# Experts' tokens normed behind their first product, second top-16 searches beside the key searches: a change to a hybrid encoder layer on one core

## The chip, the core and the metric

The kernel runs on one core of one Trainium2 chip. Time is device time in microseconds (us), the median of several timed runs. The profile is one further execution with the hardware profiler on; the engines are called as it calls them: PE (TensorE, with its weight loads as PEld), DVE (VectorE), ACT (ScalarE), POOL (GpSimd) and SP (SyncE, which issues most DMAs here).

## What is computed

One layer on 256 tokens of width 2048: an RMS norm, a combined projection, a bidirectional RWKV-7 group and a grouped-query attention group, an output projection, and then a product-key mixture of single-neuron experts, which is the part that the change touches:

```
h2 = rmsnorm(x, norm2_w)                       # 256 tokens x 2048
q = (h2 @ w_pq).reshape(T, 8, 2, 128)          # 8 heads, two halves each
s = einsum('thpc,hpnc->thpn', q, sub_keys)     # 128 keys per half
s1, i1 = top_k(s[:, :, 0], 16)                 # first searches: keys
s2, i2 = top_k(s[:, :, 1], 16)
cand = s1[..., :, None] + s2[..., None, :]     # 16 x 16 sums
best, ci = top_k(cand, 16)                     # second search
e1 = take_along_axis(i1, ci // 16); e2 = take_along_axis(i2, ci % 16)
expert = e1 * 128 + e2
gate = softmax(best)
act = gelu(h2 . u_tab[expert]) * gate
out = sum over experts of act * v_tab[expert]  # then x + out, and a last rmsnorm
```

The kernel does not gather experts. It multiplies all tokens with all 16384 rows of `u_tab`, weighs the Gelu of the result with a dense gate matrix that is zero where an expert wasn't chosen, and multiplies with all of `v_tab`.

## The kernel before, in words

The first third of the time (to about 635 us) holds the projections, the RWKV and attention groups and most of the output projection; their order comes from a scheduler, and the change does not touch it. From there on the order is written out by hand: a list `todo` of pieces, each one load of 512 KB of weights (128 partitions x 1024 values), and a function `go()` (line 764) that brings the next piece. `go()` issues loads some six pieces ahead, splits pieces three ahead, and then runs the products of the piece that is due. Splitting means that ACT rounds the raw weights to a part `wH` and that either POOL or DVE subtracts it from the raw values, which leaves `wL` (`split_piece`, line 750). Which engine subtracts is the third member of a piece. Tokens are split likewise, and three products (high x high, high x low, low x high) give a product of nearly full precision. What stands between two calls of `go()` is put on the engines' queues between the pieces. Each engine runs its own queue in order.

The pieces, in order:

1. Eight late pieces of the output projection (`late`, line 787). Behind each 128-wide chunk of `x2` (the residual, channels on partitions) ACT makes the high part of chunk times norm weight, `pH`, and DVE the remainder `pL` (`rest`, line 806). The squares go to the sum for the RMS norm.
2. 32 pieces of queries, two for each of 16 half-heads (`query`, line 821), from `pH` and `pL`, so without the token's RMS factor, which is applied to the key scores (`scores_of`, line 841) as ACT's scale. POOL subtracts. Each score block is searched by DVE for its 16 largest (`search`, line 849; `top16`, line 832: two rounds of eight maxima, their indices, and a replacement). In the same loop `h2_chunk` (line 929) makes the tokens for the experts: DVE multiplies a chunk with the norm weight and with the RMS factor spread over all partitions (`rb2`), ACT rounds it to the high half of `hh`, DVE subtracts for the low half.
3. 256 pieces of up-projection (`up`, line 856): each pair gives 128 experts x 256 tokens, in PSUM as one product of 512 columns (high and low tokens side by side) and one of 256. ACT copies the low half out into a buffer `S`, DVE adds the other half. There are 26 buffers of two such results (`NSB`).
   - Over the first 28 of these pieces (`ROUTE`) run the lookups (`route`, line 986): DVE makes the 80 sums that can hold the 16 largest of the 16 x 16, in three instructions for eight heads, searches them (the second search), finds row and column, and looks the experts' numbers up by comparing (`oh`), multiplying with a copy of the index lists that ACT spreads (`ex`), and adding in a tree of halves; then the softmax. One half of the tokens (b = 0, 1) follows the other. `turn` (line 979) transposes the residual back between pieces. POOL subtracts in this stretch, DVE in the next 64 pieces.
   - Over the 64 pieces behind these the dense gates are made (`hot`, `gate`, lines 1086 and 1097): DVE makes one-hot rows, PE multiplies them, ACT copies, SP stores them to memory.
4. 16 groups of 16 down-projection pieces (`down`, line 874), with the remaining up pieces between the first ten groups. `ready` (line 1165) prepares the next group in steps between pieces: Gelu on ACT, weighing with the gates on DVE (`weigh`), rounding on ACT, remainder on DVE (`remain`). The gates of a group are loaded back by SP (`gate_load`, line 1142). In groups 11 to 15 no up pieces are left. One piece in three is subtracted by DVE, the others by POOL.
5. The last norm and the stores (`finish`).

Of the kernel before, what the change touches and what calls it, by code (L numbers as in the profile page):

```python
# [37 lines left out]
ROUTE = 28  # L38
RSTEPS = 22
# [95 lines left out]
def body(tc, a, out, dbg={}):  # L135
# [592 lines left out]
    accp = pool("accp", side="right")  # L728
    tk = pool("tk", side="right")
    skp = pool("skp", side="right")  # L730
    x2p = pool("x2p", side="right")
    pH = x2p.tile([128, 16, 256], R, name="pH")
    pL = x2p.tile([128, 16, 256], R, name="pL")
# [53 lines left out]
    def late(m):  # L787
# [4 lines left out]
        def use(raw):  # L792
            for n in (2 * m, 2 * m + 1):
# [6 lines left out]
                act(pH[:, n], x2(n), AF.Copy, scale=Pm("n2", n))  # L800
# [5 lines left out]
    def rest(n):  # L806
        V.scalar_tensor_tensor(pL[:, n], x2(n), Pm("n2", n), pH[:, n].bitcast(F), op0=OP.mult, op1=OP.subtract)  # L807
# [45 lines left out]

    Sb, upp = {}, {}

    def up(i, j, c, eng):
        def use(H, L):
# [3 lines left out]
            for k in range(8):  # L861
                mm(p, H[:, k], hh[:, c + k].rearrange("p x t -> p (x t)"), c + k == 0, False)
                mm(p[:, 0:256], L[:, k], hh[:, c + k, 0], False, c + k == 15)
            if c:
                if not j:
                    Sb[i] = sp.tile([128, 2, 256], F, name="S")
# [39 lines left out]
    for r, (i, j, c) in enumerate(ups[:4 * NSB]):  # L906
        todo.append(up(i, j, c, V if ROUTE <= r < ROUTE + 64 else G))
# [18 lines left out]
    hh = actp.tile([128, 16, 2, 256], R, name="xy")  # L926
    hw = {}

    def h2_chunk(n):
        if n < 16:  # L930
            hw[n] = s2p.tile([128, 256], F, name="w", bufs=3)
            V.scalar_tensor_tensor(hw[n], x2(n), Pm("n2", n), rb2, op0=OP.mult, op1=OP.mult)
# [5 lines left out]
    n_h = 0  # L938
    for n in range(16):
        go()  # L940
        if n == 0:
# [288 lines left out]
```

## Time and profile before

| | us |
|---|---|
| timed runs, median of 3 (lowest to highest) | 2300.5 (2297.33 to 2303.76) |
| the profiled execution | 2296.94 |
| its span, first to last instruction | 2295.2 |
| PE busy in it | 2226.0 |
| DVE / ACT / POOL busy | 1180.9 / 936.7 / 861.7 |
| mean granted TensorE clock | 0.982 of full |

Lines of a profile that begin with two numbers are instructions in order of time: start and duration in us, engine, line of the kernel, operation, what it writes and reads, shapes, and in brackets how long the engine was idle before it and what ended that. In the chain (the work that ended last, followed back) the two numbers are start and length of a run of such work. In a stretch (`A:B`) stand its length, then the busy time and the count of PE, PEld, DVE, ACT and POOL, the granted clock, the share of the DMA engines, and GB/s. In a group stand line, engine, operation, tiles, shapes and count, then total busy us and mean ns of one, then the idle time before them. Many instructions are recorded under the lines of three helpers, 159 (`mm`), 162 (`act`) and 165 (`tt`), so they are told apart by their tiles: `wH` and `wL` are split weights, `oh` and `ee` belong to the lookups, `o` to the gates, `h<-gd` to the loading of the gates.

### The profile page before, as it was taken

Reading aid. Unit: us, or ns where it says so; the run is one execution under the profiler, and the core shown is the slowest. Engines: PE = TensorE matmul, PEld = TensorE weight load, DVE = VectorE, ACT = ScalarE, POOL = GpSimd, SP = SyncE. Lnnn points to the kernel's source line nnn. Section 1 sums busy time; section 2 is a strip of 40 time slices with the busy share of each in tenths; the row PEclk is TensorE's granted clock in tenths of the full one; section 3 lists DMA queues with packets and bytes.
Section 4 is the critical chain, followed back from the end, with each engine's and each line's share of the span. In section 5 each row is a group of like instructions: output and inputs, shape, how many; then the busy total and the mean of one; then the engine's idle time right before and its main releaser. Section 6 shows DMA issues by size and latency. Waiting matters only on the chain.

```text
span 2295.2 us, 33834 instructions
## 1 busy us (share of the span) xinstructions
PE 2226.0 (97%) x13042; PEld 1897.7 (83%) x13042; DVE 1180.9 (51%) x2498; ACT 936.7 (41%) x1350; POOL 861.7 (38%) x393
## 2 busy tenths in 40 slices
PE   8999799899999999999999999999999999999997
PEld 7888688787889878999888888888888888887786
DVE  3364865774468888888532332332322332345544
ACT  1121222223144545555544444444444444444443
POOL 0000000000036780000655555555555555555554
PEclk9999799799999999999999999999999999999999
DMA  5465364366364445666766566566566566676664
GB/s 199 147 192 167 128 193 152 104 205 190 116 204 146 156 164 194 215 217 219 226 197 209 185 206 208 185 209 209 186 203 209 187 207 196 199 224 220 207 205 134
DMA packets 188833, 431.52 MB, mean 188 GB/s; under 512 B 39680, under 2 KB 82304, under 8 KB 184448
## 3 DMA queue, kind: packets, MB, share of 16 engines
q1 hardware_dynamic: 177376, 409.96, 56.2%
q10 hardware_dynamic: 11296, 19.40, 2.5%
q8 instruction: 103, 1.69, 0.3%
q14 instruction: 58, 0.48, 0.1%
HBM read 391.55 MB, written 37.75 MB: 187 GB/s over the span
## 4 chain that ended last, share of the span: by engine, by line
PE 88%; DVE 5%; issue 2%; POOL 2%; DMA 1%; ACT 1%; SPq 0%; POOLq 0%; ACTq 0%
PE pc L159 35%; PE pj L159 32%; PE pr L159 18%; POOL wL L165 2%; PE pt L159 1%; DVE oh L165 1%; PE pr L533 0%; DVE S L165 0%; DMA h<-gd 0%; DMA cst<-cst 0%; ACT wH L162 0%; DVE pk L165 0%; DVE pL L807 0%; DVE o L1093 0%; DVE AK L165 0%
## 5 line engine op out<-in xcount | busy, mean ns | idle before, releaser
L165 POOL TENSOR_TENSOR wL<-raw,wH 128x1024 fp32r<-128x1024 f32 x344 | 836.2, 2435 | 998.4 <-ACT wH L162 990.9
L162 ACT ACTIVATE wH<-raw 128x1024 fp32r<-128x1024 f32 x544 | 575.2, 1060 | 472.2 <-PE pc L159 282.6
L165 DVE TENSOR_TENSOR wL<-raw,wH 128x1024 fp32r<-128x1024 f32 x200 | 250.3, 1252 | 369.2 <-ACT wH L162 368.9
L159 PE MATMUL pc<-wH,aL 128*128 128x512 f32 x1024 | 405.5, 396 | 0.0
L159 PE MATMUL pc<-wH,aH 128*128 128x512 f32 x1024 | 404.0, 395 | 1.2 <-DVE acc L165 1.1
L159 PE MATMUL pc<-wL,aH 128*128 128x512 f32 x1024 | 404.2, 395 | 0.0
L159 PE MATMUL pj<-xy,rw 128*128 128x256 f32 x1664 | 385.4, 388 | 0.2 <-ACT xy L162 0.2
L159 PE MATMUL pr<-xy,wH 128*128 128x512 f32 x1024 | 365.9, 399 | 2.8 <-ACT wH L162 2.8
L159 PE MATMUL pj<-xy,wH 128*128 128x512 f32 x1024 | 364.7, 398 | 0.8 <-ACT wH L162 0.8
L159 PEld LDWEIGHTS pj<-xy,rw 128*128 128x128 f32 x1664 | 318.3, 194 | 50.4 <-issue 4.7
L159 PE MATMUL pr<-xy,wL 128*128 128x256 f32 x1024 | 287.5, 281 | 2.0 <-POOL wL L165 1.9
L159 PE MATMUL pj<-xy,wL 128*128 128x256 f32 x1024 | 286.8, 280 | 1.8 <-POOL wL L165 1.0
L159 PEld LDWEIGHTS pc<-wH,aH 128*128 128x128 f32 x1024 | 192.2, 188 | 49.0 <-DVE acc L165 2.5
L159 PEld LDWEIGHTS pr<-xy,wH 128*128 128x128 f32 x1024 | 192.8, 188 | 46.5 <-ACT wH L162 3.1
L159 PEld LDWEIGHTS pc<-wL,aH 128*128 128x128 f32 x1024 | 192.2, 188 | 46.8
L159 PEld LDWEIGHTS pc<-wH,aL 128*128 128x128 f32 x1024 | 192.2, 188 | 46.1
L159 PEld LDWEIGHTS pj<-xy,wH 128*128 128x128 f32 x1024 | 192.1, 188 | 44.1 <-ACT wH L162 1.1
L159 PEld LDWEIGHTS pr<-xy,wL 128*128 128x128 f32 x1024 | 194.2, 190 | 2.6 <-POOL wL L165 2.6
L159 PEld LDWEIGHTS pj<-xy,wL 128*128 128x128 f32 x1024 | 193.4, 189 | 2.8 <-POOL wL L165 1.3
L165 DVE TENSOR_TENSOR acc<-pc,acc 128x512 f32<-128x512 f32 x128 | 86.3, 688 | 148.5 <-PE pc L159 148.5
L505 POOL COPY vp<-zv 128x256 f32<-128x256 f32 x16 | 8.0, 498 | 307.8 <-PE pr L510 178.8
L162 ACT ACTIVATE gc<-pc 128x512 f32<-128x512 f32 x64 | 68.9, 1077 | 73.6 <-PE pc L159 73.6
(298 smaller groups left out, 2308.6 us busy)
## 6 DMA issues: line engine op xcount, KB each, us to landing
raw<-u SPq DMA_DIRECT2D x256, 512.0 KB, 4.1
raw<-v SPq DMA_DIRECT2D x256, 512.0 KB, 3.9
rw<-win SPq DMA_DIRECT2D x160, 256.0 KB, 2.7
PK<-D ACTq DMA_DIRECT2D x16, 1024.0 KB, 8.1
raw<-wpq SPq DMA_DIRECT2D x32, 512.0 KB, 3.8
gd<-gc SPq DMA_DIRECT2D x16, 1024.0 KB, 4.9
h<-gd SPq DMA_DIRECT2D x32, 512.0 KB, 6.7
D<-pk SPq DMA_DIRECT2D x16, 896.0 KB, 4.5
```

The costliest lines, as they stand in the source:

```text
L159: T.matmul(o, l, r, start=start, stop=stop, skip_group_check=True)
L162: S.activation(o, i, f, **kw)
L165: e.tensor_tensor(o, x, y, op=op)
L505: G.tensor_copy(vp[:, 1:5], c4(rev(zv[:, i], d)))
```

## The change

It has four parts.

**The norm.** `h2_chunk` is gone. `hh` now holds the chunk times norm weight without the RMS factor, high and low side by side, and is written where `pH` and `pL` were. Queries use it too (`wide`: 512 columns, then 256), with the same copy and addition behind them as the up-projections. The RMS factor is applied to the up-projections' results, by a DVE multiply of 128x512 per result (`norm`), a step of `ready` ahead of the Gelu. 16 of the 26 result buffers lie in the old `xy` memory.

**The second searches.** For each head and half of the tokens ACT makes the 80 sums in nine small instructions with a bias (`sums`) as soon as both key searches are there, and DVE searches them (`second`) behind the next piece, inside the query loop.

**The lookups.** The last key and second searches and the lookups run over the first 21 up pieces, both halves of the tokens in one sequence (`both`); softmax comes first.

**Who subtracts.** DVE takes up pieces 9 to 88, before 28 to 91.

```
-ROUTE = 28
-RSTEPS = 22
+ROUTE = 21
...
-                act(pH[:, n], x2(n), AF.Copy, scale=Pm("n2", n))
+                act(hh[:, n, 0], x2(n), AF.Copy, scale=Pm("n2", n))
...
+    def wide(p, H, L, c):
+
+        for k in range(8):
+            mm(p, H[:, k], hh[:, c + k].rearrange("p x t -> p (x t)"), c + k == 0, False)
+            mm(p[:, 0:256], L[:, k], hh[:, c + k, 0], False, c + k == 15)
+
     def query(n, c):
         def use(H, L):
             if c == 0:
-                qp[n] = bank()[:, :256] if n % 2 else pp.tile([128, 256], F, name="pj")
-            for k in range(8):
-                mm3(qp[n], H[:, k], L[:, k], pH[:, c + k], pL[:, c + k], c + k == 0, c + k == 15)
+                qp[n] = bank() if n % 2 else pp.tile([128, 512], F, name="pj")
+            wide(qp[n], H, L, c)
             if c:
+                p = qp.pop(n)
                 qs[n] = s2p.tile([128, 256], F, name="q", bufs=3)
-                act(qs[n], qp.pop(n))
+                act(qs[n], p[:, 256:512])
+                tt(V, qs[n], p[:, 0:256], qs[n], OP.add)
...
-                    Sb[i] = sp.tile([128, 2, 256], F, name="S")
+                    Sb[i] = SX[0][:, i % NSB] if i % NSB < 16 else sp[0].tile([128, 2, 256], F, name="S")
...
-        todo.append(up(i, j, c, V if ROUTE <= r < ROUTE + 64 else G))
+        todo.append(up(i, j, c, V if 9 <= r < ROUTE + 68 else G))
...
-    def h2_chunk(n):
-        if n < 16:
-            hw[n] = s2p.tile([128, 256], F, name="w", bufs=3)
-            V.scalar_tensor_tensor(hw[n], x2(n), Pm("n2", n), rb2, op0=OP.mult, op1=OP.mult)
-        if 0 < n < 17:
-            act(hh[:, n - 1, 0], hw[n - 1])
-        if n > 1:
-            tt(V, hh[:, n - 2, 1], hw.pop(n - 2), hh[:, n - 2, 0].bitcast(F), OP.subtract)
...
+    def sums(h, b):
+
+        v, w = val[:, b, 2 * h], val[:, b, 2 * h + 1]
+        cd = cds[h, b] = tk.tile([128, 80], F, name="cd", bufs=3)
+        act(cd[:, 0:16], w, AF.Identity, bias=v[:, 0:1])
+        for i in range(1, 8):
+            act(cd[:, 8 + 8 * i:16 + 8 * i], w[:, 0:8], AF.Identity, bias=v[:, i:i + 1])
+        act(cd[:, 72:80], v[:, 8:16], AF.Identity, bias=w[:, 0:1])
+
+    def second():
+
+        for h, b in list(cds):
+            w = tk.tile([128, 80], F, name="mr2", bufs=2)
+            top16(best[:, b, h], bix[:, b, h], cds.pop((h, b)), w)
+        if heads:
+            sums(*heads.pop(0))
...
+    for r in range(ROUTE):
+        go()
+        second()
+        if r == 0:
+            find(13, 1)
+            scores_of(14)
+        elif r < 3:
+            find(14, r - 1)
+            if r == 1:
+                scores_of(15)
+        elif r < 5:
+            find(15, r - 3)
+        elif r < 7:
+            numbers(0, r - 5)
+        else:
+
+            for _ in range(1 + (r % 2 or r > 15)):
+                next(parts, 0)
+            if r in (12, 14):
+                numbers(1, r // 2 - 6)
...
+    def norm(g, q):
+        tt(V, Sb[4 * g + q], Sb[4 * g + q], rb2[:, None].to_broadcast([128, 2, 256]), OP.mult)
...
     def ready(g):
 
-        for q in range(4):
-            gelu(g, q)
+        for q in range(5):
+            if q < 4:
+                norm(g, q)
             yield
-            weigh(g, q)
+            if q < 4:
+                gelu(g, q)
+            if q:
+                remain(g, q - 1)
             yield
-            round_(g, q)
-            yield
-            remain(g, q)
-            yield
+            if q < 4:
+                weigh(g, q)
+                yield
+                round_(g, q)
```

What this moves on DVE shows at three places. First the query loop; one turn of it on DVE before. `w` and `xy` are the experts' tokens (scaled chunk, and `hh`, which was kept in that memory), `sc`, `val`, `idx` and `mr` belong to a key search:

```order
L932 SCALAR_TENSOR_TENSOR w<-h_3195,prm,rstdb 128x256
L165 TENSOR_TENSOR xy<-w,xy 128x256
L833 MAX val<-sc 128x8
L834 MAX_INDEX idx<-val,sc 128x8
L835 MATCH_REPLACE mr<-val,sc 128x128
L836 MAX val<-mr 128x8
L837 MAX_INDEX idx<-val,mr 128x8
```

The same place now; `q` is the query, summed from PSUM, and `cd`, `best`, `bix` belong to a second search:

```order
L164 TENSOR_TENSOR q<-pj,q 128x256
L840 MAX best<-cd 128x8
L841 MAX_INDEX bix<-best,cd 128x8
L842 MATCH_REPLACE mr_5712<-best,cd 128x80
L843 MAX best<-mr_5712 128x8
L844 MAX_INDEX bix<-best,mr_5712 128x8
L840 MAX val<-sc 128x8
L841 MAX_INDEX idx<-val,sc 128x8
L842 MATCH_REPLACE mr<-val,sc 128x128
L843 MAX val<-mr 128x8
L844 MAX_INDEX idx<-val,mr 128x8
```

Both instructions on token chunks are gone from this place, and a sum from PSUM and a second search stand beside the key search.

Second the lookups of the first half of the tokens on DVE, before; `S` is a sum of an up-projection:

```order
L165 TENSOR_TENSOR S<-pr,S 128x256
L165 TENSOR_TENSOR oh<-ix_6885,rows 128x2048
L165 TENSOR_TENSOR oh<-oh,ex_6661 128x2048
L165 TENSOR_TENSOR oh<-oh 128x8x128
L165 TENSOR_TENSOR oh<-oh 128x8x64
L165 TENSOR_TENSOR oh<-oh 128x8x32
L165 TENSOR_TENSOR ee<-oh 128x128
```

The same lookup now (the sums of the up-projections are called `xy` after their new memory):

```order
L164 TENSOR_TENSOR wL<-raw,wH 128x1024
L164 TENSOR_TENSOR oh<-ix_6853,rows 128x2048
L164 TENSOR_TENSOR wL<-raw,wH 128x1024
L164 TENSOR_TENSOR xy<-pr,xy 128x256
L164 TENSOR_TENSOR oh<-oh,ex 128x2048
L164 TENSOR_TENSOR oh<-oh 128x8x128
L164 TENSOR_TENSOR oh<-oh 128x8x64
L164 TENSOR_TENSOR oh<-oh 128x8x32
L164 TENSOR_TENSOR ee<-oh 128x128
```

The weights' subtractions, which were on POOL's queue here, stand between the steps of the lookup on DVE's.

Third the preparation of a down-projection group on DVE, before; `h` is a gate tile, `aL` the remainder of the weighed Gelu, `acc` the accumulation of a finished product:

```order
L165 TENSOR_TENSOR acc<-pc,acc 128x512 x2
L165 TENSOR_TENSOR aL<-S,aH 128x512
L165 TENSOR_TENSOR S<-S,h_15939 128x2x128
L165 TENSOR_TENSOR S<-S,h_15940 128x2x128
L165 TENSOR_TENSOR wL<-raw,wH 128x1024
```

The same place now:

```order
L164 TENSOR_TENSOR acc<-pc,acc 128x512 x2
L164 TENSOR_TENSOR xy<-xy,rstdb 128x512
L164 TENSOR_TENSOR aL<-xy,aH 128x512
L164 TENSOR_TENSOR xy<-xy,h_15787 128x2x128
L164 TENSOR_TENSOR xy<-xy,h_15788 128x2x128
L164 TENSOR_TENSOR wL<-raw,wH 128x1024
```

One multiply with the RMS factor (`rstdb`) is added in front of each remainder; everything else keeps its order.

More of the change, by code (lines that the diff above doesn't have):

```diff
@@ L860, in use @@
             p = upp[i, j]
-            for k in range(8):
-                mm(p, H[:, k], hh[:, c + k].rearrange("p x t -> p (x t)"), c + k == 0, False)
-                mm(p[:, 0:256], L[:, k], hh[:, c + k, 0], False, c + k == 15)
+            wide(p, H, L, c)
             if c:
                 if not j:
-                    Sb[i] = sp.tile([128, 2, 256], F, name="S")
+                    Sb[i] = SX[0][:, i % NSB] if i % NSB < 16 else sp[0].tile([128, 2, 256], F, name="S")
                 act(Sb[i][:, j], p[:, 256:512])
@@ L944, in body @@
         if n > 2:
-            search(n - 3, 1)
-            if n_h < 18:
-                h2_chunk(n_h)
-                n_h += 1
+            find(n - 3, 1)
         go()
+        second()
         if n == 0:
@@ L958, in body @@
             scores_of(n - 2)
-            search(n - 2, 0)
-        if n > 5 and n_h < 18:
-            h2_chunk(n_h)
-            n_h += 1
-    while n_h < 18:
-        h2_chunk(n_h)
-        n_h += 1
-    search(13, 1)
-    for n in (14, 15):
-        scores_of(n)
-        for b in range(2):
-            search(n, b)
-    close(s2p, x2p, skp)
-    sp = pool("sp", NSB)
-    hk = sp.tile([128, 3, 256], F, name="hk", bufs=1)
+            find(n - 2, 0)
+    hk = accp.tile([128, 3, 256], F, name="hk")
     ees = [tk.tile([128, 3, 128], F, name="ee", bufs=2) for _ in range(2)]
     acc = accp.tile([128, 2, 2048], F, name="acc")
+    SX.append(actp.tile([128, 16, 2, 256], F, name="xy"))
     def turn(b, c):
@@ L1038, in route, with numbers @@
             yield
[L1040 to L1047 removed]
+    exs = {}
+    def numbers(b, x):
+        exs[b, x] = tk.tile([128, 8, 16, 16], BF, name="ex", bufs=2)
+        act(exs[b, x], idx[:, b].rearrange("p (h x) k -> p h x k", x=2)[:, :, x, :, None].to_broadcast([128, 8, 16, 16]))
     def route_end(b):
@@ L1059, in body, with both @@
         G.memset(shift[:, i:i + 1], v)
-    routes = [route(b) for b in range(2)]
-    for b in range(2):
-        half = ROUTE // 2
-        done = 0
-        for r in range(half):
-            go()
-            if r % 3 == 2:
-                turn(b, r // 3)
-            while done * (half - 2) < (r + 1) * RSTEPS:
-                next(routes[b], 0)
-                done += 1
-            if b and r == 1:
-                route_end(0)
-        for _ in routes[b]:
-            pass
+    def both():
+        for b in range(2):
+            yield from route(b)
+    parts = both()
+    for r in range(ROUTE):
+        go()
+        second()
+        if r == 0:
[14 more added lines that the diff above has]
+                numbers(1, r // 2 - 6)
+        if r > 4 and r % 2 == 0:
+            turn((r - 6) // 8, (r - 6) % 8 // 2)
+        if r == 15:
+            route_end(0)
+    for _ in parts:
+        pass
     go()
+    turn(1, 3)
     go()
     route_end(1)
-    close(tk)
+    close(s2p, skp, tk)
+    sp.append(pool("sp", NSB - 16))
     gp = pool("gp", side="right")
@@ L1165, in ready @@
     def ready(g):
-        for q in range(4):
-            gelu(g, q)
+        for q in range(5):
+            if q < 4:
+                norm(g, q)
             yield
-            weigh(g, q)
+            if q < 4:
+                gelu(g, q)
+            if q:
+                remain(g, q - 1)
             yield
-            round_(g, q)
-            yield
-            remain(g, q)
-            yield
+            if q < 4:
+                weigh(g, q)
+                yield
+                round_(g, q)
     go()
     gate_load(0)
-    for q in range(4):
+    for q in range(5):
         go()
-        gelu(0, q)
+        if q < 4:
+            norm(0, q)
+        if q:
+            gelu(0, q - 1)
     for q in range(4):
```

57 lines of the change are left out of this document (23 added, 34 removed).

## Prediction

> **What bounds the kernel now.** I read the page first, then the waits and the chain, then the timeline of the two stages that the change touches, then the groups by shape. The page:
>
> ```profile
> span 2295.2 us, 33834 instructions
> PE 2226.0 (97%) x13042; PEld 1897.7 (83%) x13042; DVE 1180.9 (51%) x2498; ACT 936.7 (41%) x1350; POOL 861.7 (38%) x393
> ```
>
> PE is the bound: it idles 69 us in all, and the change takes no column of its work away. So a gain can only be idle or stretched PE time in the stages that are rewritten (queries, lookups, gates, down-projections), and a loss can only be a new wait of PE there. The start of each query's score product, the last one before the lookups and the first gate product (PE's timeline):
>
> ```profile
> 698.50 0.27 PE L159 MATMUL pc<-skT,q 128*128 128x128 f32 x1
> ...
> 735.22 0.27 PE L159 MATMUL pc<-skT,q 128*128 128x128 f32 x1
> ...
> 768.27 0.27 PE L159 MATMUL pc<-skT,q 128*128 128x128 f32 x1
> ...
> 774.38 0.27 PE L159 MATMUL pc<-skT,q 128*128 128x128 f32 x1
> ...
> 877.67 0.27 PE L159 MATMUL pc<-o,o 128*128 128x128 f32 x1
> ```
>
> Six queries from 698.50 to 735.22 take 6.12 us each, the four to 768.27 take 8.26: 4 x 2.14 = 8.6 us lost. The loop behind that, in the timeline of all engines:
>
> ```profile
> 722.07 2.30 DVE L932 SCALAR_TENSOR_TENSOR w<-h,prm,rstdb 128x256 f32<-128x256 f32 x1
> ...
> 724.40 0.42 ACT L162 ACTIVATE xy<-w 128x256 fp32r<-128x256 f32 x1 [2.77 <-DVE w L932]
> ...
> 725.85 2.40 POOL L165 TENSOR_TENSOR wL<-raw,wH 128x1024 fp32r<-128x1024 f32 x1 [1.76 <-ACT wH L162]
> ...
> 726.20 2.33 DVE L932 SCALAR_TENSOR_TENSOR w<-h,prm,rstdb 128x256 f32<-128x256 f32 x1
> ```
>
> DVE's norm of a token chunk (L932) starts just behind POOL's subtraction and ends just after it (728.53 against 728.25); ACT's copy waits for it; ACT's next rounding of weights stands behind that copy; POOL's next subtraction waits for the rounding. One turn is POOL's 2.40 and the 1.76 that it waits, 4.16 us a piece; PE needs 6.12 / 2 = 3.06. PE lives on its three pieces in hand until 735, then loses.
>
> The lookups: 877.67 - 774.38 = 103.3 us hold 31 pieces, 8 turns, three score products and two transposes of the lookups' results. In the chain:
>
> ```profile
> 680.53 5.68 PE pj L159 x48
> ...
> 768.43 0.46 PE pc L159 x4
> ...
> 794.47 0.44 PE pc L983 x4
> 794.90 5.66 PE pr L159 x32
> ...
> 831.10 0.33 PE pc L1052 x3
> ```
>
> 31 x 2.83 + 8 x 0.44 + 3 x 0.46 + 2 x 0.33 = 93.3, so 10.0 us are lost. DVE's timeline there shows the same lookup twice, once while POOL subtracts and once while POOL is idle:
>
> ```profile
> 804.14 3.31 DVE L165 TENSOR_TENSOR oh<-oh,ex 128x2048 bf16<-128x2048 bf16 x1
> 807.48 7.71 DVE L165 TENSOR_TENSOR oh<-oh 128x1024 bf16<-128x1024 bf16 x3
> ...
> 815.43 1.22 DVE L165 TENSOR_TENSOR oh<-ix,rows 128x2048 bf16<-128x2048 bf16 x1
> ...
> 816.90 1.22 DVE L165 TENSOR_TENSOR oh<-oh,ex 128x2048 bf16<-128x2048 bf16 x1
> 818.15 1.48 DVE L165 TENSOR_TENSOR oh<-oh 128x1024 bf16<-128x1024 bf16 x3
> 819.66 0.29 DVE L165 TENSOR_TENSOR ee<-oh 128x128 f32<-128x128 bf16 x1
> ...
> 820.53 0.29 DVE L1045 TENSOR_REDUCE gs<-ee 128x8 f32<-128x128 f32 x1 [0.38 <-ACT ee L162]
> ```
>
> 3.31 against 1.22, 7.71 against 1.48. PE's stalls follow, and one brings a slow clock (the stretch 820 to 840; mean clock 0.91, so some 1.8 of the 10.0 us):
>
> ```profile
> 820.00:840.00 20.00, 16.57 (x86) 14.27 (x87) 15.62 (x54) 14.31 (x18) 18.00 (x8) 0.91 0.49 160
> ```
>
> **The change part by part.** Groups by shape, then two searches of each length (128 and 80 entries) by their first instructions:
>
> ```profile
> L165 DVE TENSOR_TENSOR S<-pj,S 128x256 f32<-128x256 f32 x64 | 27.1, 424 | 131.9 <-ACT S L162 131.7
> L833 DVE MAX8 val<-sc 128x8 f32<-128x128 f32 x32 | 9.0, 281 | 8.0 <-ACT sc L162 8.0
> ...
> L162 ACT ACTIVATE wH<-raw 128x1024 fp32r<-128x1024 f32 x544 | 575.2, 1060 | 472.2 <-PE pc L159 282.6 <-issue 138.7 <-PE pr L159 24.4
> L162 ACT ACTIVATE sc<-pc,rstd 128x128 f32<-128x128 f32 x32 | 9.8, 363 | 2.6 <-DVE mr L835 1.9
> L162 ACT ACTIVATE Pc<-Pt 128x4 f32<-128x4 f32 x16 | 3.1, 194 | 0.0
> ```
>
> ```profile
> 687.31 0.30 DVE L833 MAX8 val<-sc 128x8 f32<-128x128 f32 x1 [2.73 <-ACT sc L162]
> ...
> 688.90 0.28 DVE L833 MAX8 val<-sc 128x8 f32<-128x128 f32 x1
> ...
> 786.98 0.23 DVE L833 MAX8 best<-cd 128x8 f32<-128x80 f32 x1
> ...
> 788.30 0.22 DVE L833 MAX8 best<-cd 128x8 f32<-128x80 f32 x1
> ```
>
> *Query loop, norm out and second searches in.* The 16 scalings, roundings and subtractions of chunks go, and the 4.16 us loop with them. What DVE now holds per two queries: two sums from PSUM (0.42 each), four searches (688.90 - 687.31 = 1.59) and two second searches (788.30 - 786.98 = 1.32): 9.8 us of PE's 12.2. The means 424 ns and 281 ns over all instructions, nearly all beside POOL, say that these forms are not held up. ACT: four roundings 4.2, two copies 0.8 (0.42 at 724.40), four score copies 1.5, and 18 small sums. Their form is not in the trace; the smallest ACT copy is 194 ns, the 128-wide score copy 363: 3.5 to 6.5 us, so 10.0 to 13.0 of 12.2. I take 194, since the sums have 8 or 16 elements and the other row has 128. Behind a sum on ACT's queue stand the score copies and the next rounding; PE's three pieces (9 us) cover them. Gain 8.6 us, 0 at worst.
>
> *Query products as 512 + 256 columns.* 48 products took 5.68 us, 32 of the new form take 5.66 in the lookups: 0.02 x 16 = 0.3 us gained; I take 0.8, between 0 and 2. The Trainium skill (TensorE: Matmul & The Clock Gate, Back-to-back issue gap) gives each isolated product a fixed 2.5 ns; by that estimate 256 fewer products save 0.6 us, and no row here isolates that figure.
>
> *Lookups.* POOL's last subtraction is now piece 8; from piece 9 DVE subtracts. So lookups run at the unheld times, but DVE carries 15 subtractions over lookup pieces 6 to 20. Sum on DVE: 15 x 1.21 (the row at 2083.34, below) = 18.2; 8 sums 3.4; two second searches 2.6; four lookups of 1.22 + 1.22 + 1.48 + 0.29 = 4.2, 16.8; softmax and index steps, 18 instructions of 0.29 at most, 5.2. Together 46 us; PE's time for these pieces with 8 turns is 15 x 2.83 + 8 x 0.44 = 46. These durations overlap by a tenth (the first step starts at 815.43 and lasts 1.22, yet with a 0.42 us sum between them the second starts at 816.90), so DVE is at 90 to 100%. The heavy steps lie last (pieces 17 to 19), three pieces in hand cover 8.5 us, and two pieces without lookups follow. Of 10.0 lost I keep 1.5; bounds 0 and 7. The two scalings by ACT of index lists wait for DVE's earlier lookup; behind them stand ACT's roundings, under the same cover. Gain 8.5.
>
> *Gates.* The waits of PE between 600 and 1150 hold one for the gates, at their end, where POOL subtracts again:
>
> ```profile
> PE pc L159 <- DVE o L1093: 1.1, 1, 1.1
> ```
>
> With the stretch starting seven pieces earlier DVE keeps the subtractions until the last gate's operands are made. Gain 1.1, bounds 0 and 1.2. SP's raw loads keep their order; the gate stores and loads move seven pieces ahead, with more room before they are used.
>
> *The norm at the down-projections.* New on DVE: 64 multiplies of 128x512, both inputs in SBUF, four per group, and ACT's Gelu waits for each. The same shape in the trace, and the weighings next to it:
>
> ```profile
> 2080.02 0.69 DVE L165 TENSOR_TENSOR acc<-pc,acc 128x512 f32<-128x512 f32 x1 [0.71 <-PE pc L159]
> 2080.63 2.79 DVE L165 TENSOR_TENSOR aL<-S,aH 128x512 fp32r<-128x512 f32 x1
> 2083.34 1.21 DVE L165 TENSOR_TENSOR wL<-raw,wH 128x1024 fp32r<-128x1024 f32 x1
> 2084.48 5.17 DVE L165 TENSOR_TENSOR S<-S,h 128x256 f32<-128x256 f32 x2
> ...
> 2205.51 0.68 DVE L165 TENSOR_TENSOR aL<-S,aH 128x512 fp32r<-128x512 f32 x1
> ```
>
> ```profile
> 2057.70:2102.80 45.10, 44.45 (x191) 35.48 (x190) 30.10 (x26) 20.95 (x24) 26.47 (x11) 1.00 0.73 232
> ```
>
> Free it costs 4 x 0.68 = 2.7 us a group, held 4 x 2.79 = 11.2. DVE's fullest group is busy 30.1 of 45.1 us (columns: PE, PE loads, DVE, ACT, POOL), so either fits; what is left is position. The Trainium skill (SBUF — State Buffer, Who interferes with whom) states that a DVE instruction with two SBUF inputs and a GpSimd one that reads SBUF exclude each other for a whole instruction. By that the norm is held wherever it meets a subtraction; the 2.79 against 0.68 agrees, and so do the lookups. Off the path in the ten groups that have up-projections beside them (32 pieces for 14 steps); in the last five I charge 0.4 us each, 2.0 in all. Bounds: 1.1 gained (the 0.65 us lost in this group, and nearly as much elsewhere, since the first weighing now comes a piece later after its load) and 12 lost.
>
> **Sum.** -8.6 - 0.8 - 8.5 - 1.1 + 2.0 = -17.0 us against the profiled execution's 2296.94: 2279.9. That execution lies at the lowest of the three timed runs (2297.33), 3.6 under their median 2300.5; I expect the new median some 2 us over the like, 2282.
>
> **Rivals.**
> 1. *The norm starves PE.* If every multiply, remainder and weighing of the last five groups is held, three pieces' work on DVE is 2.79 + 2.79 + 5.17 + 1.21 + 1.5 x 0.69 = 13.0 us against 3 x 2.82 (45.10 / 16) = 8.5: 4.5 over, four times a group, 18, less 8.5 in hand and 4.1 that the two pieces without steps leave: some 5.5 us a group lost, 28 in five. With 2.0 of it in my sum: 2282 + 26 = 2308. It overtakes the kernel before from 4.1 us a group on, with three in four of these steps held. For it: the 0.65 us stall in a group that already has such a row of held steps. Against: DVE is free 15 us in that group, the fullest. 8%.
> 2. *ACT's sums take the loop's place.* 18 sums at 363 ns bring ACT to 13.0 of 12.2 us, and since they wait for searches, the period stays near 8: the 8.6 us come back, and with late searches some 1.5 of the lookups: 2292, no change by my bound. Against: 194 ns. 10%.
> 3. *DVE is full in the lookups.* Waits between ACT and DVE (0.38 at 820.53) add up on an engine at 100%, and PE loses 7 us there, not 1.5: 2287.5, still faster. 14%.
>
> **Chances.** Forecast 68%, about 2275 to 2286 by itself. A measurement of this kernel tells some 0.3% (6.9 us, below 2293.6) from no change. Faster: 68 + 14 = 82%; same 10%; slower 8%. The range goes from the gains at their upper bounds (8.6 + 2 + 10 + 1.2 + 1.1 = 22.9: 2274) to just over rival 2, 2294; it leaves out the slower rival and little else.
>
> **What would show it.** Right: score products 6.1 us apart through all queries; lookups of about 1.2 and 1.5 us throughout; the stretch 820 to 840 at full clock; PE idle near 50 us. Wrong: PE waiting for POOL's remainder behind ACT's sums (rival 2), for DVE's remainder between queries and gates (rival 3), or norm multiplies with a mean near 2.8 us and PE waits for DVE after 2000 us (rival 1).

## The result, and the profile after

The changed kernel takes 2278.1 us (median of 6 runs, 2276.4 to 2284.0) against 2299.6 for the kernel before in the same number of runs: ratio 0.9911, 95% interval 0.9894 to 0.9928. The forecast was 2282, within 2274 to 2294. The profiled execution took 2277.42 us, 19.5 less than that of before (2296.94).

The page after; PE stays the bound:

```profile
span 2275.6 us, 33493 instructions
PE 2214.7 (97%) x12790; PEld 1883.2 (83%) x12790; DVE 1223.4 (54%) x2556; ACT 961.8 (42%) x1479; POOL 823.6 (36%) x377
```

Of the 19.6 us of span, only 8.3 were idle time of PE (69.2 before, 60.9 now); 11.3 were busy time. So PE is not only idle less; its products also take less time (3.8 us less busy time in the queries, 2.2 in the lookups and the pieces up to the down-projections, 4.4 in the down-projections). The marks of the stages on PE's timeline, first before, where the prediction does not show them, then after (first late output product, first and fourteenth score product, first and last gate, first and last down-projection product):

```profile
634.37 0.89 PE L159 MATMUL pj<-xy,raw 128*128 128x256 f32 x3 [2.05 <-DMA raw<-wout]
...
686.26 0.39 PE L159 MATMUL pc<-skT,q 128*128 128x128 f32 x2
...
1110.33 1.05 PE L159 MATMUL pc<-o,o 128*128 128x128 f32 x8
...
1138.96 0.39 PE L159 MATMUL pc<-wH,aH 128*128 128x512 f32 x1
...
2282.87 0.40 PE L159 MATMUL pc<-wH,aL 128*128 128x512 f32 x1
```

```profile
635.62 0.67 PE L158 MATMUL pj<-xy,raw 128*128 128x256 f32 x2 [2.37 <-DMA raw<-wout]
...
688.40 0.61 PE L158 MATMUL pc<-skT,q 128*128 128x128 f32 x4
...
766.34 0.61 PE L158 MATMUL pc<-skT,q 128*128 128x128 f32 x4
...
844.33 0.46 PE L158 MATMUL pc<-o,o 128*128 128x128 f32 x2 [0.74 <-DVE o L1108]
...
1075.86 1.06 PE L158 MATMUL pc<-o,o 128*128 128x128 f32 x8
...
1123.91 0.40 PE L158 MATMUL pc<-wH,aH 128*128 128x512 f32 x1
...
2263.35 0.40 PE L158 MATMUL pc<-wH,aL 128*128 128x512 f32 x1
```

These marks give the table (us). The gates are counted to the start of the last product of their last group, 1111.11 before and 1076.64 now. Seven up pieces that stood ahead of the gates now stand behind them, so the two lines beside "(both)" at the lookups are one sum:

| stretch | before | after | difference | in my sum |
|---|---|---|---|---|
| start to the first late piece | 634.37 | 635.62 | +1.25 | 0 |
| to the first score product | 51.89 | 52.78 | +0.89 | - |
| 13 queries | 88.12 | 77.94 | -10.18 | -9.4 (both) |
| lookups, to the first gate (31 pieces, now 24) | 103.29 | 77.99 | (both, next line) | |
| last gate to the down-projections (7 more pieces now) | 27.85 | 47.27 | -5.88 (both) | -8.5 |
| gates | 233.44 | 232.31 | -1.13 | -1.1 |
| down-projections with the rest of the up pieces | 1143.91 | 1139.44 | -4.47 | +2.0 |
| rest | 12.3 | 12.2 | -0.1 | 0 |

The first row is no effect of the change: over the fourteen profiles of this study that mark lies between 632.2 and 639.0, in a part that all have alike. Behind it the stretches repeat: the gates take 232.2 to 232.3 us in all nine profiles built on the changed kernel. So effects of one us are read from the stretches below; the timed medians carry the first part's scatter.

The lookups on DVE after run at the unheld durations all through, 1.21 and 1.48:

```profile
805.66 1.21 DVE L164 TENSOR_TENSOR oh<-oh,ex 128x2048 bf16<-128x2048 bf16 x1
806.91 1.48 DVE L164 TENSOR_TENSOR oh<-oh 128x1024 bf16<-128x1024 bf16 x3
...
812.38 1.21 DVE L164 TENSOR_TENSOR oh<-oh,ex 128x2048 bf16<-128x2048 bf16 x1
813.62 1.48 DVE L164 TENSOR_TENSOR oh<-oh 128x1024 bf16<-128x1024 bf16 x3
...
816.48 0.28 DVE L164 TENSOR_TENSOR ee<-best 128x128 f32<-128x128 f32 x1
820.37 1.23 DVE L164 TENSOR_TENSOR wL<-raw,wH 128x1024 fp32r<-128x1024 f32 x1 [3.61 <-ACT wH L161]
```

But DVE then stands idle for 3.61 us, until ACT has rounded a weight. ACT in the same stretch:

```profile
806.91 1.91 ACT L161 ACTIVATE ex<-idx 128x2048 bf16<-128x2048 uint32 x1 [3.08 <-DVE oh L164]
...
810.42 1.06 ACT L161 ACTIVATE wH<-raw 128x1024 fp32r<-128x1024 f32 x1
816.80 0.31 ACT L161 ACTIVATE ee<-ee 128x128 f32<-128x128 f32 x1 [5.32 <-DVE ee L164]
...
819.29 1.05 ACT L161 ACTIVATE wH<-raw 128x1024 fp32r<-128x1024 f32 x1
```

ACT waits 5.32 us for `ee<-best`, the subtraction ahead of the second half's exponential, which stands on DVE's queue behind two lookups. The next rounding stands behind the exponential. PE's waits between the fourteenth score product and the gates:

```profile
PE pr L158 <- DVE wL L164: 1.4, 3, 0.8
PE pc L1048 <- DVE ee L164: 1.3, 2, 0.9
PE pc L158 <- DVE o L1108: 0.7, 1, 0.7
PE pr L158 <- ACT wH L161: 0.2, 1, 0.2
```

Of these, 0.2 for a rounding and 0.8 for the subtraction behind it come at 825 to 827, after ACT's long wait. The 0.9 for `ee` is another thing: at 815.48, while ACT still waits, PE stands at the transposes of the first half's results, which are placed at a fixed piece, until DVE has finished the second lookup (815.13 + 0.29). From 814 to 829 us DVE was busy 8.8 of 15.0 us, so it was not full there; it waited for ACT as ACT had waited for it.

With my own yardstick (24 x 2.83, nine turns x 0.44, since the change repeats one, 3 x 0.46, 2 x 0.33: 73.9) the lookups lose 4.1 us, not 1.5.

The norm at the down-projections has two groups of instructions, as its results lie in two pools:

```profile
L164 DVE TENSOR_TENSOR xy<-xy,rstdb 128x512 f32<-128x512 f32 x40 | 30.2, 756 | 0.0
...
L164 DVE TENSOR_TENSOR S<-S,rstdb 128x512 f32<-128x512 f32 x20 | 13.9, 696 | 0.0
```

Means of 756 and 696 ns: of these 60, one alone is held, and it is the one that begins near the start of a subtraction by POOL, 0.17 us after it:

```profile
2110.98 2.52 POOL L164 TENSOR_TENSOR wL<-raw,wH 128x1024 fp32r<-128x1024 f32 x1 [0.36 <-ACT wH L161]
...
2111.15 2.89 DVE L164 TENSOR_TENSOR xy<-xy,rstdb 128x512 f32<-128x512 f32 x1
```

The other 59 take 0.68 to 0.88 us. They begin while POOL is idle or in the last 0.33 us of its subtraction.

Then the up pieces between two down-projection groups, 16 in each stretch, which I had not looked at. Two neighbouring stretches before, then two after (length, then busy time and count of PE, PE loads, DVE, ACT, POOL, clock):

```profile
1184.05:1228.43 44.38, 44.38 (x258) 39.12 (x256) 13.04 (x21) 21.18 (x27) 25.73 (x11) 1.00 0.62 194
1273.22:1318.45 45.23, 45.23 (x258) 39.21 (x257) 14.02 (x21) 21.18 (x27) 24.99 (x11) 1.00 0.57 184
```

```profile
1168.72:1213.10 44.38, 44.38 (x258) 39.06 (x257) 16.13 (x22) 20.58 (x26) 26.02 (x11) 1.00 0.61 194
1257.89:1302.26 44.37, 44.37 (x257) 39.07 (x256) 15.03 (x22) 20.58 (x26) 25.09 (x11) 1.00 0.61 188
```

PE is busy to the last 10 ns in all four, at full clock, with the same products, and yet every second stretch of before is 0.85 us longer (four of nine, and the half stretch at the end by 0.4). After, none is.

### The profile page after: what moved, and what is told of

Read it like the earlier page. It is cut to its first block, busy times and chain, and to the rows that moved or that the text cites. A ratio compares the mean times of both kernels' runs of the same rounds, so it can differ in the third digit from the quotient of the medians.

```text
span 2275.6 us, 33493 instructions
## 1 busy us (share of the span) xinstructions
PE 2214.7 (97%) x12790; PEld 1883.2 (83%) x12790; DVE 1223.4 (54%) x2556; ACT 961.8 (42%) x1479; POOL 823.6 (36%) x377
## 4 chain that ended last, share of the span: by engine, by line
PE 91%; DVE 5%; ACT 1%; DMA 1%; issue 1%; ACTq 0%; SPq 0%; DVEq 0%
PE pc L158 37%; PE pj L158 33%; PE pr L158 19%; PE pt L158 1%; DVE wL L164 1%; DVE oh L164 1%; ACT wH L161 0%; PE pr L532 0%; DMA VV<-V 0%; DVE pk L164 0%; DVE xy L164 0%; DVE hh L807 0%; DVE AK L164 0%; DVE h L164 0%; DVE rs L164 0%
## 5 line engine op out<-in xcount | busy, mean ns | idle before, releaser
L164 POOL TENSOR_TENSOR wL<-raw,wH 128x1024 fp32r<-128x1024 f32 x328 | 798.3, 2438 | 1018.5 <-ACT wH L161 1011.9
L164 DVE TENSOR_TENSOR wL<-raw,wH 128x1024 fp32r<-128x1024 f32 x216 | 274.1, 1269 | 347.4 <-ACT wH L161 347.3
L158 PE MATMUL pr<-hh,wH 128*128 128x512 f32 x1152 | 409.3, 396 | 0.2 <-ACT wH L161 0.2
L158 PE MATMUL pj<-hh,wH 128*128 128x512 f32 x1152 | 408.0, 395 | 1.5 <-DVE hh L807 1.3
L158 PE MATMUL pr<-hh,wL 128*128 128x256 f32 x1152 | 323.1, 281 | 1.4 <-DVE wL L164 1.4
L158 PE MATMUL pj<-hh,wL 128*128 128x256 f32 x1152 | 322.1, 280 | 0.0
L158 PEld LDWEIGHTS pj<-hh,wH 128*128 128x128 f32 x1152 | 216.4, 188 | 48.4 <-DVE hh L807 2.0
L158 PEld LDWEIGHTS pr<-hh,wH 128*128 128x128 f32 x1152 | 217.2, 189 | 46.6 <-ACT wH L161 0.5
L158 PEld LDWEIGHTS pr<-hh,wL 128*128 128x128 f32 x1152 | 217.2, 189 | 2.4 <-DVE wL L164 2.4
L158 PEld LDWEIGHTS pj<-hh,wL 128*128 128x128 f32 x1152 | 216.5, 188 | 0.4
```

What stands on the lines that cost most here:

```text
L158: T.matmul(o, l, r, start=start, stop=stop, skip_group_check=True)
L164: e.tensor_tensor(o, x, y, op=op)
```

## The experiments

### Queries: the late copy, and the RMS factor in PSUM

The prediction said that the late queries lose time in a loop POOL, DVE, ACT, POOL. The first run cuts it where ACT waits, in the kernel before:

```
+        if n > 2:
+            tt(V, hh[:, n - 3, 1], hw.pop(n - 3), hh[:, n - 3, 0].bitcast(F), OP.subtract)
         if n < 16:
             ...
-        if 0 < n < 17:
-            act(hh[:, n - 1, 0], hw[n - 1])
-        if n > 1:
-            tt(V, hh[:, n - 2, 1], ...)
+        if 1 < n < 18:
+            act(hh[:, n - 2, 0], hw[n - 2])
```

> The kernel before, with ACT's copy of a token chunk put one call later (and the remainder with it), so that the copy no longer waits for the scaling that DVE has just begun. Theory A, the loop POOL, DVE, ACT, POOL sets the late queries: the loop is cut, score products stay near 6.1 us apart for at least most of the last four intervals, and 4 to 8.6 us come back: 2290 to 2295. Theory B, DVE itself, held by POOL for 2.3 us at each of its two-input instructions, is too slow whatever ACT waits for: the late intervals stay near 8.3, within 2 us of the kernel before.

Measured: 2302.0 us, ratio to before 1.0017 (1.0006 to 1.0027); score products late in the queries 8.8 us apart instead of 8.26. One turn, in time:

```profile
723.54 2.69 POOL L165 TENSOR_TENSOR wL<-raw,wH 128x1024 fp32r<-128x1024 f32 x1 [1.76 <-ACT wH L162]
723.56 0.41 DVE L165 TENSOR_TENSOR xy<-w,xy 128x256 fp32r<-128x256 f32 x1
...
724.00 2.51 DVE L934 SCALAR_TENSOR_TENSOR w<-h,prm,rstdb 128x256 f32<-128x256 f32 x1
726.54 0.42 ACT L162 ACTIVATE xy<-w 128x256 fp32r<-128x256 f32 x1 [2.30 <-DVE w L934]
```

The copy stands one call later on ACT's queue and still starts just behind a scaling: DVE has fallen one call further behind. It even costs some 0.28 us more a turn, about what POOL's subtraction takes longer where the remainder (0.41) begins with it, 2.69 for 2.40. So putting the copy one call later does not cut the loop, and Theory A of this run fell; the slow intervals are also longer than Theory B said. What was left is the 2.5 us of the scaling. The second run shortens that alone, again in the kernel before:

```
-            V.scalar_tensor_tensor(hw[n], x2(n), Pm("n2", n), rb2, op0=OP.mult, op1=OP.mult)
+            V.scalar_tensor_tensor(hw[n], x2(n), Pm("n2", n), pb[0], op0=OP.mult, op1=OP.mult)
...
-            psb = bank("pc")[:, :256]
-            spread(psb, rstd2.to_broadcast([128, 2, 128]))
-            act(rb2, psb)
+            pb.append(bank("pt")[:, :256])
+            spread(pb[0], rstd2.to_broadcast([128, 2, 128]))
```

> The kernel before, with the scaling of a token chunk on DVE reading the RMS factor from PSUM instead of SBUF (sums with one input in PSUM took 0.42 us beside POOL, this scaling 2.3). The run with the later copy did not cut the loop: ACT's copy still began 0.03 us behind a scaling, one call later. Theory A, what makes the late queries slow is that the scaling is held until POOL's subtraction ends: unheld it takes 0.4 to 0.8 us, the late score products come 6.1 us apart again, and 8 to 8.6 us come back, 2290 to 2292. Theory B, this form is held all the same, or DVE and ACT wait for each other whatever it takes: the four late intervals stay near 8.3, within 2 us of the kernel before.

Measured: 2291.6 us, ratio 0.9968 (0.9955 to 0.9982). All thirteen intervals are 6.11 to 6.13 us, the queries take 79.57 us for 88.12. The same place:

```profile
719.65 4.96 POOL L165 TENSOR_TENSOR wL<-raw,wH 128x1024 fp32r<-128x1024 f32 x2 [1.17 <-ACT wH L162]
...
720.25 0.46 DVE L932 SCALAR_TENSOR_TENSOR w<-h,prm,pt 128x256 f32<-128x256 f32 x1
720.63 1.71 DVE L165 TENSOR_TENSOR xy<-w,xy 128x256 fp32r<-128x256 f32 x1
720.75 0.42 ACT L162 ACTIVATE xy<-w 128x256 fp32r<-128x256 f32 x1 [1.18 <-DVE w L932]
```

With one input in PSUM the scaling takes 0.46 us in the middle of POOL's work, where 2.3 stood. The remainder, both inputs in SBUF, is still held (1.71), and ACT's copy still waits for the scaling; neither costs PE anything. So what makes the loop slow is the held scaling, and this small change to the kernel before gives the 8.6 us of the queries by itself (the timed median is 7.0 lower, with the scatter of the first part in it). The Trainium skill (SBUF — State Buffer, Who interferes with whom) states that a DVE instruction with at most one SBUF input, outside the modes that use both ports, does not contend with GpSimd; the 0.46 agrees.

### Queries: three products, and doubled sums

```
-            wide(qp[n], H, L, c)
+            for k in range(8):
+                mm3(qp[n][:, 0:256], H[:, k], L[:, k], hh[:, c + k, 0], hh[:, c + k, 1], c + k == 0, c + k == 15)
...
-                act(qs[n], p[:, 256:512])
-                tt(V, qs[n], p[:, 0:256], qs[n], OP.add)
+                act(qs[n], p[:, 0:256])
```

> The changed kernel with the queries multiplied as three products of 256 columns again, copied out by ACT alone (DVE's sum from PSUM goes). Theory A, the two-product form saves 0.12 us a query: score products 6.12 us apart instead of 6.00, 1.9 us in all, so about 2280. Theory B, the form is worth what I put down for it, 0.3 to 0.8 us: score products at most 6.05 apart.

Measured: 2278.1 us. Score products come 6.08 and 6.14 us apart in turn, so the two-product form does save 0.11 a query, about as Theory A says. But the stretch ahead of the first score product is back at 51.92 us from 52.78. The wide product needs both halves of a token chunk, so PE waits 1.3 us for the last chunks' low halves where it waits 0.7 for a high and a low half here; and a wait of 0.9 for the RMS factor, which the changed kernel has ahead of the first score product, is gone here. From the first late piece to the down-projections the form gains 488.86 - 488.29 = 0.6 us net, near what I had put down; the timed medians are equal.

```
+        for _ in range(2):
             act(cd[:, 0:16], w, AF.Identity, bias=v[:, 0:1])
             ...
```

> The changed kernel with each of ACT's small sums for the second searches executed twice. ACT is busy 58.6 of 77.9 us between the first and the fourteenth score product. Theory A, my second rival is one doubling away: 117 more sums in that stretch at the 0.2 us from start to start of two of them bring ACT to 81 us, so score products come 6.2 to 6.4 us apart and 2.5 to 5 us are lost, 2281 to 2283. Theory B, the pieces in hand and ACT's slack take it: score products stay 6.0 apart, within 1 us of 2278.

Measured: 2297.9 us, all of the gain gone; the first to the fourteenth score product takes 89.3 us, in intervals of about 6.0 and, four times, 7.85 to 10.2; up to the first gate another 8.1 us are lost (86.08 for 77.99). Neither theory had the size. ACT after the doubling, then POOL:

```profile
723.67 0.61 ACT L161 ACTIVATE sc<-pc,rstd 128x128 f32<-128x128 f32 x2
724.17 1.06 ACT L161 ACTIVATE wH<-raw 128x1024 fp32r<-128x1024 f32 x1
727.49 3.57 ACT L161 ACTIVATE cd<-val 128x16 f32<-128x16 f32 x18 [2.27 <-DVE val L843]
730.97 1.05 ACT L161 ACTIVATE wH<-raw 128x1024 fp32r<-128x1024 f32 x1
```

```profile
732.10 2.39 POOL L164 TENSOR_TENSOR wL<-raw,wH 128x1024 fp32r<-128x1024 f32 x1 [2.38 <-ACT wH L161]
```

ACT is not full (74.6 of the 89.3 us). But a batch of sums waits 2.27 us for DVE's search and then takes 3.57, and the rounding behind it begins 5.7 us after the last one ended. POOL waits 2.38 us for that rounding, and PE waits 7.8 us in all for POOL's remainders between 688 and 790 us. My second rival was priced by ACT's load; as these rows read, what decides is the length of a batch behind a wait. The Trainium skill (ScalarE: Activation LUTs, What ACT_TABLE_LOAD costs) gives about 280 ns plus 0.833 an element to an instruction with a bias from memory, and an overlap of 93 ns between neighbours; the 18 sums in 3.57 us, 0.19 from start to start, agree.

### Lookups: who subtracts

In the changed kernel POOL again, up to piece 27; then in the kernel before DVE, from piece 9:

```
-        todo.append(up(i, j, c, V if 9 <= r < ROUTE + 68 else G))
+        todo.append(up(i, j, c, V if 28 <= r < ROUTE + 68 else G))
```

> The changed kernel with POOL subtracting up to up piece 27 instead of 8, so the lookups run beside POOL again. Theory A, who subtracts is what freed the lookups: their steps are held again (near 3.3 and 7.7 us for 1.2 and 1.5), PE loses 5 to 10 us more there, 2283 to 2288. Theory B, the new sequence and the earlier second searches are what shortened this stage: within 2 us of 2278.1.

Measured: 2294.6 us, ratio to before 0.9989 (0.9979 to 0.9998); from the fourteenth score product to the first gate it takes 15.5 us longer than the changed kernel. DVE's steps, and PE's wait there:

```profile
807.90 3.43 DVE L164 TENSOR_TENSOR oh<-ix,rows 128x2048 bf16<-128x2048 bf16 x1
...
836.14 3.32 DVE L164 TENSOR_TENSOR oh<-oh,ex 128x2048 bf16<-128x2048 bf16 x1
```

```profile
PE pc L1048 <- DVE ee L164: 15.8, 3, 7.8
```

The steps are held again, as Theory A says, but the price is another: PE's queue holds the transposes of the results at a fixed piece, and PE stands there 15.8 us in three waits. In the shorter sequence of the change, 21 pieces for 28, held lookups cost 15.5 us, more than Theory A allowed.

```
-        todo.append(up(i, j, c, V if ROUTE <= r < ROUTE + 64 else G))
+        todo.append(up(i, j, c, V if 9 <= r < ROUTE + 64 else G))
```

> The kernel before, with DVE subtracting from up piece 9 instead of 28, nothing else. Theory A, who subtracts is the whole gain of the lookups: lookup steps of 1.2 and 1.5 us, 6 to 10 us less between the last query's score product and the first gate product (103.3 us before). Theory B, the sums of the 80 and the second searches are still there, DVE is full: at most 3 us less.

Measured: 2293.6 us, ratio 0.9977 (0.9968 to 0.9987). Between the fourteenth score product and the first gate 97.91 us for 103.29, 5.4 less, and 1.3 more in the gates. Between the two theories: from the fourteenth score product to the down-projections, gates included, this edit gains 4.1 us (360.47 for 364.58) and the change 7.0 (357.57). So who subtracts gives more than half of that by itself; the rest needs the new sequence.

### Lookups: order or load

```
+        for k in range(0 if b else 2):
+            gt = ees[k][:, 2].rearrange("p (h k) -> p h k", h=8)
+            tt(V, gt, best[:, k], best[:, k, :, 0:1].to_broadcast([128, 8, 16]), OP.subtract)
+            act(gt, gt, AF.Exp)
...
-        if r == 15:
+        if r == 17:
             route_end(0)
```

> The changed kernel with the softmax's subtraction and exponential of the second half of the tokens done together with the first half's, and the transposes of the first half's results two pieces later. The lookups of the changed kernel lost some 4 us of PE, not 1.5. Theory A, part of it is order on the queues: ACT stands 5.3 us (811.5 to 816.8) in front of an exponential that waits for DVE behind two lookups, with weight roundings behind it, and PE waits 1.2 us for transposes of numbers that DVE has not finished: 2 to 3 us come back, 69 us from the last score product to the first gate product for 71.55. Theory B, DVE is simply full over these pieces: the waits reappear at the end of the stage, less than 1 us comes back.

Measured: 2276.1 us; from the last score product to the first gate 68.03 us for 71.55, 3.5 less. (The first query of that profile fell on a lower clock, 0.66, and lost 1.6 us, which the time shows and the stretch doesn't.) Theory A, and above its range: DVE does the same work, and most of the loss of 4.1 goes with the order. The edit moves two things, the exponential and the transposes, and no run parts them. By PE's waits in the changed kernel, 1.3 us stood at the transposes and 1.6 at split weights; here the first are gone and 0.5 of the second is left, and PE has no wait from 814 to 829 us, where it had 1.9.

```
-ROUTE = 21
+ROUTE = 24
...
-            for _ in range(1 + (r % 2 or r > 15)):
+            for _ in range(1 + (r < 12)):
                 next(parts, 0)
-            if r in (12, 14):
-                numbers(1, r // 2 - 6)
+            if r in (15, 18):
+                numbers(1, r // 3 - 5)
```

(with the steps of both halves up to the index lists ahead of all lookups, `route_end(0)` at piece 19, and without the ninth turn)

> The changed kernel with the softmax and index steps of both halves first, two a piece, then one lookup step a piece over 24 pieces instead of 21, and without the ninth, repeated transposition of the residual. Theory A, DVE's density over pieces 10 to 20 is the rest of the loss: 3 to 4.5 us come back against the changed kernel from the first score product to the first down-projection (435.5 us there), 2273.5 to 2275. Theory B, the total of DVE's work to the first gates is what binds, so spreading gives no more than moving the exponential.

Measured: 2274.2 us; from the first score product to the down-projections 430.17 us for 435.51, 5.3 less, above the range of Theory A. The run with the early exponential takes 433.64 there, 432.1 without its slow first query. So spreading gives up to 1.9 us more than that order alone, of which the turn that is left out can be 0.4.

### The norm

```
     def norm(g, q):
-        tt(V, Sb[4 * g + q], Sb[4 * g + q], rb2[:, None].to_broadcast([128, 2, 256]), OP.mult)
+        return
```

> The changed kernel without the 64 norm multiplies at the down-projections (the RMS factor is left out of the experts' first product; everything else stays). Theory A, the norm is hidden behind PE and the 4.5 us that the down-projections gained came from elsewhere (PE's products ran 7 ns a step slower in every second group of the kernel before, some 0.84 us in each of four groups): the time stays within 1.2 us of the changed kernel's 2278.1, and its groups with up-projections keep 89.2 us. Theory B, the norm has a price of about the 2 us that I charged, and the gain elsewhere covers it: 2275 to 2276.5, with the wait of PE for the accumulation near 2073 us gone.

Measured: 2278.8 us; down-projections 1139.10 us for 1139.44. The difference of 0.34 us lies in one of the late groups (46.19 us with it, 45.86 without). The groups with up pieces take 89.16 to 89.19 us in both. Theory A. Even the 0.34 is not shown to be the norm's: the run with the queries as three products has the norm, and that group takes 45.86 there too. So the norm costs nothing that these profiles can tell.

```
     def norm(g, q):
         tt(V, Sb[4 * g + q], Sb[4 * g + q], rb2[:, None].to_broadcast([128, 2, 256]), OP.mult)
+        tt(V, Sb[4 * g + q], Sb[4 * g + q], rb2[:, None].to_broadcast([128, 2, 256]), OP.mult)
```

> The changed kernel with each norm multiply executed twice (the RMS factor is applied twice). Theory A, DVE has room: 64 more multiplies of 0.7 to 2.8 us stay off the path in the ten groups with up-projections, and the five late groups lose at most 0.5 us each: 2278 to 2281. Theory B, position on DVE's queue decides as in my first rival: the late groups lose 2 to 5 us each, 2288 to 2303.

Measured: 2287.1 us, ratio 0.9948 (0.9931 to 0.9964). PE's waits from the last gates on:

```profile
PE pc L158 <- DVE acc L164: 4.6, 5, 1.2
PE pj L158 <- POOL wL L164: 1.9, 2, 1.7
```

The second set of 64 costs 4.8 us in the down-projections (the groups without up pieces lose 1.1, 0.8, 0, 1.1 and 1.7) and 2.4 where the first group is prepared, 7.2 in all, where the first set cost 0.34 at most. Between the theories in size: the mechanism of my first rival exists, one norm away, at 1 us a late group.

### PE's pace

```
+    mm(bank("pc")[:, 0:128], ident, ident)
     for g in range(16):
         nxt = ready(g + 1) if g < 15 else iter(())
```

> The kernel before, with one more product of 128 columns on PE (its result is not used) ahead of the first down-projection group. In the kernel before every second group of 32 pieces takes 90.02 us and the others 89.18, the slow ones because the 512-column products of the up-projections start 236 ns before what follows them instead of 230; the changed kernel has no slow groups. Theory A, that pace is a state of PE's stream, set by what went before: the extra product changes which groups are slow, or how many. Theory B, it is where the operands lie in memory or which buffers a group uses: the same groups stay at 90.02 us. The time moves by at most 3.5 us.

Measured: 2299.5 us, ratio 1.0003 (0.9992 to 1.0015). The first two stretches of up pieces now:

```profile
1181.57:1226.79 45.22, 45.22 (x257) 39.24 (x256) 13.04 (x21) 21.19 (x27) 25.71 (x11) 1.00 0.60 191
1271.59:1315.98 44.39, 44.39 (x258) 39.13 (x257) 14.02 (x21) 21.19 (x27) 25.08 (x11) 1.00 0.58 189
```

The first is the slow one and the second the fast one, and so on in turn: one product swapped them, at no change of the up pieces' memory or buffers (the extra product takes one turn of the three `pc` buffers, which the up pieces do not use). The run with the factor in PSUM, also built on the kernel before, has them swapped too. Theory A, as far as it goes: the pace depends on what went before on PE. What in it decides stays open. By their starts in the kernel before, both forms are slower in a slow stretch, not the 512-column products alone: on average 233.4 ns for 230.0 from such a product to the next, and 119.8 for 116.7 from one of 256 columns.

### The start of the queries

On top of the lookups over 24 pieces:

```
-    todo += [query(n, c) for n in range(16) for c in (0, 8)]
+    todo += [query(n, c) for c in (0, 8) for n in range(2)] + [query(n, c) for n in range(2, 16) for c in (0, 8)]
...
+        if n == 1:
+            square_sum(15)
...
-        if n == 0:
-            square_sum(15)
...
-        if n == 2:
+        if n == 5:
             psb = bank("pc")[:, :256]
```

(the square sum, and the reciprocal root behind it, now stand between the two pieces of their turn)

> The kernel with lookups over 24 pieces, and the start of the queries reordered: the first halves of queries 0 and 1 go ahead of their second halves, the last square sum comes one piece later, and the RMS factor is spread over the partitions at query 5 instead of 2. PE waited there 0.84 and 1.06 us for the low halves of the last token chunks, 1.54 for the last square sum and 1.17 for the factor, and ran for some 3 us at a lower clock. Theory A, these waits are order alone and go: 3 to 6 us less than with lookups over 24 pieces, 2268.5 to 2271. Theory B, the chain from the last output projection to the token chunks is what binds and PE waits for it at another place: within 1.5 us of 2274.

Measured: 2268.8 us, ratio to before 0.9864 (0.9848 to 0.9881), 9.3 us below the changed kernel. The stretch ahead of the first score product takes 49.45 us for 53.02 with the lookups over 24 pieces, and the clock between 662 and 690 us is 1.00 for 0.94. Of the four waits that the expectation names, PE has one left (the profile of the run over 24 pieces puts the four at 1.3 for the two halves together, 1.3 and 0.9):

```profile
PE pc L158 <- DVE sm L810: 0.5, 1, 0.5
```

Theory A. The stretch gives 3.6 us; the rest of the 5.4 between the two medians lies in no stretch that this edit touches. This is the fastest version of the study.

## Why the prediction was right

The sign, the range and the likeliest case held. That the sum of -17.0 came so near -19.5 is in part luck: it holds errors of both signs that nearly cancel. The lookups and the first part were 3.9 us worse than in the sum, the down-projections 6.5 better.

- **Query loop (-8.6).** Measured right, and -9.3 with the form and the longer start. The loop is as described; what makes it slow is the scaling held by POOL, by the run with the factor in PSUM, in which ACT's copy still waits for the scaling and costs PE nothing. ACT's sums fitted for a reason that was luck: I priced them at 194 ns, the time of another copy, but each takes 288 ns and starts 0.19 us after the one before:

```profile
L161 ACT ACTIVATE cd<-val 128x8 f32<-128x8 f32 x128 | 26.1, 288 | 0.0
```

- **Query form (-0.8).** 0.11 us a query, some 1.5 over 13, less 0.9 at the start, where PE waits for the chunks' low halves and the RMS factor. Those waits were not in my sum.
- **Lookups (-8.5).** Measured -5.9. The step that failed: "behind them stand ACT's roundings, under the same cover". Three pieces in hand (8.5 us) did not cover waits of ACT of 3.1 and 5.3 us within 13 us. The loss kept was 4.1, not 1.5. I summed DVE's load over the whole stretch, 46 of 46 us, and took the exponential for a small step, but it stands behind two lookups. I also had the heavy steps at pieces 17 to 19; that holds for the second half of the tokens, and the first half's lookups run at pieces 10 to 13, with that exponential and PE's transposes right behind them. My third rival, DVE full, had 7 us, and in the main the wrong ground: DVE was idle 6.2 of the 15 us from 814 to 829, and the order gives back 3.5.
- **Gates (-1.1).** Measured -1.13.
- **Norm (+2.0).** Measured 0.34 at most, inside its bounds. That a multiply is held where it meets a subtraction is so (2.89 us), but one in 60 did. How often they meet was the term that I had too high.
- **Not foreseen (some -4.2).** The down-projections gained 4.47 us. The two groups with stalls give 0.3 of it (45.72 and 45.57 us before, 46.19 and 44.80 now). PE's pace gives the rest, with no wait: 3.8 in the up pieces and 0.3 in the first group. It stood in the trace of before (44.38 and 45.23 us in turn), and my working took it as given.
- **Against my signs.** Score products, lookup steps and the clock in 820 to 840 (1.00) came as said. PE idle near 50 us did not: it was 60.9. More than a third of the queries' and lookups' gain and nearly all of the down-projections' lay in busy time, and the first part, which the change does not touch, was idle 1.8 us longer in that profile.

## What to carry to other kernels

When DVE and POOL share a stage, find the DVE instruction with two SBUF inputs that others wait for, and give it an input in PSUM, or give POOL's work to DVE there; here the first way, a handful of lines, was worth 8.6 us. A sum of an engine's load tells whether it fits, not whether it fits in order: look for each cross-engine wait that has the pacing engine's next input behind it on the same queue, and compare its length with the cover. And compare equal stretches of the bound engine with each other before pricing what lies between them.

## What the runs showed of the hardware

The same 16 pieces took PE 44.38 or 45.23 us, at full clock with no wait, in turn, and one extra product of 128 columns swapped the turns; in nine profiles built on the changed kernel all such stretches took the shorter time. What in PE's stream sets the pace is not known.

From 632 to 704 us, in the three profiles named here, a low clock stood only right behind waits of PE, wherever these lay, but not behind every wait. The changed kernel waited 0.57, 0.78 and 1.26 us between 670 and 674 us, and its clock was 0.62 and 0.82 in the two stretches of 3 us from 674 on. The run with the early exponential had the same three waits and kept 1.00 behind them; it waited 2.57 us for the RMS factor, and its clock was 0.71 and 0.72 from 689 to 695. The version with the reordered start had only 0.5 and 0.3 us of waits between 662 and 690 us, and 1.00 throughout; behind a wait of 2.17 us for a DMA, which ended at 636.74, its clock was 0.50 from 638 to 641. Behind a wait of 2.37 us at the same mark the changed kernel kept 1.00. No run shows what decides.
